# Parts of four layer 1 weight chunks made in layer 0 and kept in memory

## The chip, the cores and the metric

One core of a Trainium2 chip runs the kernel. The metric is device microseconds of one execution; lower is better. The kernel before takes 521.77 us, the median of three runs (521.5 to 522.45).

## The reference

Two residual layers over x of 512 tokens by 1024 channels, in fp32. What matters here:

```python
# layer 0: FoX (8 heads with a forget-gate bias) and MoBA (8 heads), head width 64
h = rms_norm(x, norm_g);  proj = h @ w_in          # q, k, v of both, forget logits, gate
logits = q k^T / 8 + c[query] - c[key]             # FoX: c is the running sum of log-sigmoid forget gates
out = softmax(masked logits) v                     # causal; MoBA: own block and chosen blocks
x = x + (concat(out_fox, out_moba) * silu(gate)) @ w_out
# layer 1: conformer convolution
val, glu, z = split(rms_norm(x, g) @ w_in, 3)      # 1024 channels each
u = causal depthwise conv of width 31 over (val * sigmoid(glu)), plus bias
x = x + (silu(layer_norm(u)) * silu(z)) @ w_out
```

## The kernel before

Each dense product is made in fp32 quality from split operands: a weight chunk of 1024 x 256 (1 MB) is held as hi, rounded to fp32r, and lo, the rest, and PE runs three passes (hi hi, hi lo, lo hi). There are 36 weight chunks in one list. Chunks 0 to 15 are layer 0's q, k, v and gate, 16 to 19 its output projection, 20 to 27 are layer 1's value and GLU gate, 28 to 31 its z, 32 to 35 its output projection, used in the order 33, 34, 32, 35.

`fetch(i)` loads a chunk by SP's queue into one of two buffers `wst` (L152). `split(i)` makes hi and lo: in most chunks of layer 0 ACT copies to hi (L173) and DVE or Pool subtracts in eight pieces (L177). In chunks named in `DMAS`, lo is made by an ACT negation of the whole chunk (L175) and a DMA on Pool's queue that accumulates the raw chunk into it (L179); in chunks named in `CAST`, hi is a casting DMA on Pool's queue (L169). Only Pool's queue casts or accumulates here. hi and lo go to `whi` and `wlo` (two buffers each), or to `wx` (four buffers). Chunk 32, the late one, has its lo in the place `gh` (L160, L161), and its hi is loaded with a cast by Pool's queue near the end (L1051). `ahead(n)` splits the next chunk and then fetches the next.

Layer 0 runs dense work (64 units: one token tile of a q, k or v chunk, or half of a gate chunk) between 64 attention tiles: 8 pairs of heads, of which pairs 0 to 3 are MoBA and 4 to 7 FoX, each with 2 heads and 4 query tiles. A tile is s (two matmuls, L510 and L512), p with bias and row maximum on DVE (L522), exp on ACT (L523), transposes on PE (L526) and copies back by ACT or DVE (L534, L536). A pair ends with the matmuls by v (L603) and a product with the reciprocal sums `rb`, which come back through memory (L546, L549, L608). A FoX head's bias tile `cb`, 128 x 512, is loaded by SP (L582) into one of two buffers and its diagonal pieces are masked by Pool (L518). Gate chunks end with a tanh (L626) and two DVE products (L623, L627). `ot` holds the attention's output, eight slots of 128 x 512; `e` is the tanh's buffer.

Layer 1 convolves tile by tile: of the 31 taps DVE takes most (L766), and the rest are a product on ACT (L775) that Pool adds (L776); L783 joins the two sums, PE transposes (L796), DVE gathers statistics (L798, L903, L904), Pool takes a power for the LayerNorm (L905 lnr), DVE normalises (L911 ctok), and PE transposes again (L922) ahead of the output projection. `POOLT` is the number of taps of ACT and Pool by channel block of 128 x 512, for blocks 0 to 5; `POOLH` the same for half tiles of blocks 6 and 7. z chunks run on PE (L370 to L372) meanwhile.

The order of instructions on each engine is fixed when the program is built, by a scheduler that goes by its own estimates of cost; each engine then runs its list in order, waiting on semaphores.

## Time and profile before

| | before |
|---|---|
| median of the runs | 521.77 us (521.5 to 522.45) |
| profiled execution, time and span | 522.39 us, 520.6 us |
| PE busy | 503.7 us, 97% |
| DVE busy | 373.0 us, 72% |
| ACT busy | 329.1 us, 63% |
| POOL busy | 232.6 us, 45% |
| moved by DMA | 79.05 MB |

The page gives busy time and, by line and shape, groups of instructions with the idle time ahead of them and the instruction that ended it. Stretches of time show which engine is full where; a timeline lists one engine's instructions with start, length and, in brackets, idle time ahead and its releaser. Here is the span in 40 equal slices of 13 us; a digit is tenths of a slice, a 9 being 90% or more:

```profile
PE   8999999999999999999999999999999999769997
DVE  7745677676465577596685256999999997868741
ACT  4945678777645775576384735998676765377230
POOL 5264852020422233223101113879988985687200
DMA  8742222302122242402219668488999799962111
```

PE's lower digits stand at about 440 to 470 us; Pool and the DMA engines are little used in the first half (layer 0) and full in layer 1.

### The profile page before, as it was taken

Reading aid. Unit: us, or ns where it says so; the run is one execution under the profiler, and the core shown is the slowest. Engines: PE = TensorE matmul, PEld = TensorE weight load, DVE = VectorE, ACT = ScalarE, POOL = GpSimd, SP = SyncE. Lnnn points to the kernel's source line nnn. Section 1 sums busy time; section 2 is a strip of 40 time slices with the busy share of each in tenths; the row PEclk is TensorE's granted clock in tenths of the full one; section 3 lists DMA queues with packets and bytes.
Section 4 is the critical chain, followed back from the end, with each engine's and each line's share of the span. In section 5 each row is a group of like instructions: output and inputs, shape, how many; then the busy total and the mean of one; then the engine's idle time right before and its main releaser. Section 6 shows DMA issues by size and latency. Waiting matters only on the chain.

```text
span 520.6 us, 9754 instructions
## 1 busy us (share of the span) xinstructions
PE 503.7 (97%) x3694; PEld 459.9 (88%) x3694; DVE 373.0 (72%) x788; ACT 329.1 (63%) x668; POOL 232.6 (45%) x255
## 2 busy tenths in 40 slices
PE   8999999999999999999999999999999999769997
...
DVE  7745677676465577596685256999999997868741
ACT  4945678777645775576384735998676765377230
POOL 5264852020422233223101113879988985687200
...
DMA  8742222302122242402219668488999799962111
GB/s 293 318 145 81 84 81 83 102 24 83 61 102 94 82 111 99 144 14 108 102 52 395 130 205 242 82 211 286 235 306 259 212 270 305 262 170 105 41 51 42
DMA packets 16566, 79.05 MB, mean 152 GB/s; under 512 B 1988, under 2 KB 4352, under 8 KB 8712
## 3 DMA queue, kind: packets, MB, share of 16 engines
q1 hardware_dynamic: 12632, 51.08, 27.1%
q0 software_dynamic: 3744, 27.26, 22.0%
...
## 4 chain that ended last, share of the span: by engine, by line
PE 70%; DMA 8%; POOL 7%; ACT 6%; DVE 4%; issue 3%; SPq 0%; POOLq 0%; ACTq 0%
PE mm L361 29%; POOL pacc L776 6%; PE mm L370 6%; PE mm L371 6%; PE mm L372 6%; DMA wst<-in_w_dram 5%; PE st L361 4%; PE o L603 3%; PE tp L526 3%; PE o L361 2%; PE s L510 2%; PE s L512 2%; DMA wlo<-wst 1%; DMA xt<-in_xt_dram 1%; PE s L361 1%
## 5 line engine op out<-in xcount | busy, mean ns | idle before, releaser
L776 POOL TENSOR_TENSOR pacc<-pacc,tm 128x256 f32<-128x256 f32 (+1 forms) x125 | 120.7, 986 | 15.8 <-ACT tm L775 10.1
L766 DVE SCALAR_TENSOR_TENSOR s<-u,parts,s 128x256 f32<-128x256 f32 (+1 forms) x211 | 108.1, 569 | 0.5
L361 PE MATMUL mm<-wlo,hhi 128*128 128x256 f32 (+1 forms) x352 | 98.7, 287 | 0.8 <-DVE wlo L177 0.5
L361 PE MATMUL mm<-whi,hhi 128*128 128x256 f32 (+1 forms) x352 | 98.4, 287 | 0.0
L361 PE MATMUL mm<-whi,hlo 128*128 128x256 f32 (+1 forms) x352 | 98.3, 286 | 0.0
L775 ACT ACTIVATE tm<-u,parts 128x256 f32<-128x256 f32 (+1 forms) x125 | 66.2, 571 | 14.5 <-POOL pacc L776 14.0
L361 PEld LDWEIGHTS mm<-wlo,hhi 128*128 128x128 f32 x352 | 65.8, 190 | 2.0 <-DVE wlo L177 0.8
L361 PEld LDWEIGHTS mm<-whi,hhi 128*128 128x128 f32 x352 | 65.6, 189 | 0.7 <-issue 0.2
L361 PEld LDWEIGHTS mm<-whi,hlo 128*128 128x128 f32 x352 | 65.9, 190 | 0.2
L177 POOL TENSOR_TENSOR wlo<-wst,whi 128x512 fp32r<-128x512 f32 (+1 forms) x22 | 31.0, 1423 | 57.4 <-ACT whi L173 57.4
L173 ACT ACTIVATE whi<-wst 128x512 fp32r<-128x512 f32 (+2 forms) x77 | 49.4, 707 | 5.9 <-DMA wst<-in_w_dram 2.7
L518 POOL TENSOR_TENSOR cb<-cb,mask 128x128 f32<-128x128 f32 x32 | 15.5, 490 | 80.7 <-DVE nm L522 46.2
L523 ACT ACTIVATE p<-p,nm 128x128 f32<-128x128 f32 (+3 forms) x64 | 35.7, 559 | 24.1 <-DVE nm L522 23.6
L177 DVE TENSOR_TENSOR wlo<-wst,whi 128x512 fp32r<-128x512 f32 (+1 forms) x50 | 39.8, 830 | 9.0 <-PE o L361 7.1
L370 PE MATMUL mm<-nhi,wx 128*128 128x256 f32 (+1 forms) x104 | 33.0, 318 | 0.0
L371 PE MATMUL mm<-nlo,wx 128*128 128x256 f32 (+1 forms) x104 | 32.2, 309 | 0.0
L372 PE MATMUL mm<-nhi,wx 128*128 128x256 f32 (+1 forms) x104 | 31.9, 307 | 0.0
L371 PE MATMUL mm<-nlo,whi 128*128 128x256 f32 (+1 forms) x104 | 31.8, 307 | 0.0
L372 PE MATMUL mm<-nhi,wlo 128*128 128x256 f32 (+1 forms) x104 | 31.7, 306 | 0.0
L370 PE MATMUL mm<-nhi,whi 128*128 128x256 f32 (+1 forms) x104 | 31.7, 307 | 0.0
L526 PE MATMUL tp<-identf,p 128*128 128x128 f32 x160 | 28.4, 275 | 1.1 <-ACT p L523 0.7
L396 POOL TENSOR_TENSOR rq<-vq,mhalf 128x16 f32<-128x16 f32 x8 | 26.2, 3272 | 6.2 <-DVE vq L394 6.1
...
## 6 DMA issues: line engine op xcount, KB each, us to landing
wst<-in_w_dram SPq DMA_DIRECT2D x33, 1024.0 KB, 5.0
wx<-wst POOLq DMA_DIRECT2D x13, 1024.0 KB, 7.2
wlo<-wst POOLq DMA_DIRECT2D x8, 1024.0 KB, 8.4
whi<-wst POOLq DMA_DIRECT2D x3, 1024.0 KB, 4.5
...
```

What stands on the lines that cost most here:

```text
L173: A.activation(hi[:, ks], st[:, ks], AF.Copy)
L177: (V if eng is G and parts == 4 and k % 4 and V0 else eng).tensor_tensor(lo[:, ks], st[:, ks], hi[:, ks].bitcast(F32), op=ALU.subtract)
L361: T.matmul(po, a[:, k, ts], b[:, k, :n], start=first and i == 0, stop=last and i == len(prods) - 1)
L370: T.matmul(po, whi[:, k, cs], a, start=k == 0, stop=False)
L371: T.matmul(po, whi[:, k, cs], b, start=False, stop=False)
L372: T.matmul(po, wlo[:, k, cs], a, start=False, stop=k == KC - 1)
L396: G.tensor_tensor(r, v, mhalf[:, :16].rearrange("p (t h) -> p t h", t=NT), op=ALU.pow)
L523: A.activation(p[:, :w], p[:, :w], AF.Exp, bias=nm, scale=-1.0, accum_out=sm[:, h, t:t + 1])
L526: T.transpose(tp[:, j * P:(j + 1) * P], p[:, j * P:(j + 1) * P], identf)
L766: V.scalar_tensor_tensor(acc[:, o], v, w, first[0][:, :n] if i == 1 else acc[:, o], op0=ALU.mult, op1=ALU.add)
L775: A.activation(tm[:, :n], v, AF.Copy, scale=w)
L776: G.tensor_tensor(pacc[:, o], pacc[:, o], tm[:, :n], op=ALU.add)
```

## The change

Chunks 30 to 33 (`PRE`) are no longer fetched and split in layer 1. In layer 0 each of them is taken in four quarters of 128 x 512, 16 in all, in 18 steps (`quarters`): a step is taken when the dense unit count reaches the next entry of `UNITS`, from 20 to 40. Step n issues, all on Pool: for item n - 2 the subtraction raw - hi and two DMAs that store hi and lo to memory (`pre`), and for item n two DMAs that load the quarter raw and cast to fp32r. The first instruction of a step is made to depend on ACT's evacuation of the last dense unit (`unit[0]`), and the others are chained behind it. The steps use three pairs of places in turn: two pairs of slots of `ot`, and a pair with the tags `e` (one buffer) and `cb` (two buffers). Altogether 16 subtractions and 64 DMAs of 256 KB are added to Pool's list in layer 0.

In layer 1, SP loads the ready hi and lo by plain DMAs of 1 MB each (`load_part`). 34 and 35 follow 29 in the order of fetches. 32's hi is now loaded by SP, too. `POOLT` gives blocks 2 to 5 one tap more on ACT and Pool each, so DVE has four taps of 128 x 512 less.

```diff
--- before.py
+++ after.py
@@ -29,9 +29,9 @@
 BIG = 1e30
 WC = 256
 WPAD = 260
-POOLT = [10, 11, 12, 11, 10, 11]
+POOLT = [10, 11, 13, 12, 11, 12]
 POOLH = {(6, 0): 10, (7, 0): 10, (6, 1): 16, (7, 1): 15}
-DMAS = (20, 21, 22, 23, 24, 25, 26, 27, 28, 29, 30, 31, 32, 33, 34, 35)
+DMAS = (20, 21, 22, 23, 24, 25, 26, 27, 28, 29, 34, 35)
 APARTS = 1
 TMB = 6
 NU = 3
@@ -66,9 +66,13 @@
     return nc.vector
 
 
-CAST = (22, 26, 27, 28, 30, 31, 33, 34, 35)
+CAST = (22, 26, 27, 28, 34, 35)
 PB = 4
 PTB = 4
+
+
+PRE = range(30, 34)
+UNITS = (20, 22, 24, 25, 26, 27, 28, 29, 30, 31, 32, 33, 34, 35, 36, 37, 38, 40)
 STK = 1
 PTS = 3 * P
 NLATE = 2
@@ -154,12 +158,6 @@
 
     def split_w(w, ring, eng, parts, cast):
         st, n = w
-        if ring == "late":
-            lo = l1p[0].tile([P, KC * WC], F32R, tag="gh", name="lo", bufs=1)
-            lo = lo.rearrange("p (k n) -> p k n", k=KC)
-            A.activation(lo, st, AF.Copy, scale=-1.0)
-            G.dma_start(lo.bitcast(F32), st, accum_op=ALU.add)
-            return None, lo
         if ring == "main":
             hi, lo = flat(main, F32R, "whi", n, 2), flat(main, F32R, "wlo", n, 2)
         else:
@@ -225,11 +223,28 @@
     raw, wts = {}, {}
 
     def fetch(i):
-        if i < len(wsrc):
+        if i < len(wsrc) and i not in PRE:
             raw[i] = load_w(*wsrc[i], 4 if i == 0 else 1)
 
+    pre = {i: dram.tile([2, P, KC * WC], F32, name=f"pre{i}") for i in PRE}
+
+    def load_part(i, j, x):
+        SY.dma_start(x.bitcast(F32).rearrange("p k n -> p (k n)"), pre[i][j])
+        return x
+
+    def load_parts(i):
+
+        if rings[i] == "late":
+            lo = l1p[0].tile([P, KC * WC], F32R, tag="gh", name="lo", bufs=1)
+            return None, load_part(i, 1, lo.rearrange("p (k n) -> p k n", k=KC))
+        pool, tags, bufs, wide = (main, ("whi", "wlo"), 2, WPAD) if rings[i] == "main" else \
+            (l1p[0], ("wx", "wx"), 4, WC)
+        return tuple(load_part(i, j, flat(pool, F32R, tags[j], WC, bufs, wide)) for j in range(2))
+
     def split(i):
-        if i < len(wsrc):
+        if i in PRE:
+            wts[i] = load_parts(i)
+        elif i < len(wsrc):
             wts[i] = split_w(raw.pop(i), rings[i], SPLIT_ENG(i, nc), APARTS if i in DMAS else 4 if i == 0 or 17 <= i < 24 else WPARTS, i in CAST)
 
     fetch_xt(0, 2)
@@ -372,6 +387,8 @@
+    unit = [None]
@@ -384,7 +401,7 @@
             po = mmbank() if i > 1 or t < 2 else sbank() if i == 0 else stbank() if t == 2 \
                 else bank("o", 1)
             tok_mm(po[:, :WC], WC, hhi, hlo, t, w, i == 0)
-            A.activation(raw_t[:, t, :], po[:, :WC], AF.Copy, scale=rinv[:, t:t + 1])
+            unit[0] = A.activation(raw_t[:, t, :], po[:, :WC], AF.Copy, scale=rinv[:, t:t + 1])
             sq = sqs[:, t % 2]
             A.activation(sq, po[:, :WC], AF.Square, scale=rinv[:, t:t + 1])
             V.reduce_sum(ss[:, t, :], sq.rearrange("p (h d) -> p h d", h=4), axis=AX.X)
@@ -419,7 +436,8 @@
             tok_mm(po[:, :n], n, hhi, hlo, t, w)
             c0 = 0 if c == 0 else (260 if n == 260 else WC)
             m = min(n, 512 - c0)
-            A.activation(vt[grp][:, t, c0:c0 + m], po[:, :m], AF.Copy, scale=rinv[:, t:t + 1])
+            unit[0] = A.activation(vt[grp][:, t, c0:c0 + m], po[:, :m], AF.Copy,
+                                   scale=rinv[:, t:t + 1])
             if m < n:
                 V.tensor_scalar(zf[:, t, :], po[:, m:n], rinv[:, t:t + 1], None, op0=ALU.mult)
             if t == NT - 1 and n > m:
@@ -623,9 +641,42 @@
             V.tensor_tensor(g, po, rbc, op=ALU.mult)
 
             e = at.tile([P, S], F32, tag="e", name="e", bufs=1)
-            A.activation(e, g, AF.Tanh)
+            unit[0] = A.activation(e, g, AF.Tanh)
             V.scalar_tensor_tensor(g, e, 1.0, g, op0=ALU.add, op1=ALU.mult)
             yield
+
+    QC = KC * WC // 4
+    behind = mybir.DependencyInfo(mybir.DependencyClass.Sync, mybir.DependencyReason.DATA)
+
+    def quarters(places, parts):
+
+
+        on_way = []
+        for n, (i, q) in enumerate(parts + [(None, None)] * 2):
+            mine = []
+            def then(f, *a, **k):
+                with tc.issue_after(mine[-1].ins) if mine else nullcontext():
+                    mine.append(f(*a, **k))
+
+            if n >= 2:
+                i0, q0, st, hi = on_way.pop(0)
+                then(G.tensor_tensor, st, st, hi, op=ALU.subtract)
+                for j, x in enumerate((hi, st)):
+                    then(G.dma_start, pre[i0][j][:, q0 * QC:(q0 + 1) * QC], x)
+            if i is not None:
+                st, hi = places[n % 3]
+                src = w_ap(*wsrc[i], q * KC // 4, KC // 4)
+                then(G.dma_start, st, src)
+                then(G.dma_start, hi.bitcast(F32R), src)
+                on_way.append((i, q, st, hi))
+            tc.add_manual_dep(mine[0].ins, unit[0].ins.name, behind)
+            yield
+
+    steps = list(UNITS)
+    presplit = quarters(((ot[:, 0], ot[:, 1]), (ot[:, 2], ot[:, 3]),
+                         (at.tile([P, S], F32, tag="e", name="pst", bufs=1),
+                          at.tile([P, S], F32, tag="cb", name="phi", bufs=2))),
+                        [(i, q) for i in PRE for q in range(4)])
 
     def dense():
         for i, f, a in ((0, qk_chunk, (("moba", "q", 0), 0)), (1, qk_chunk, (("moba", "k", 0), 1)),
@@ -658,6 +709,9 @@
         while done < min(n, 64):
             next(dn, None)
             done += 1
+            if steps and steps[0] <= done:
+                steps.pop(0)
+                next(presplit)
 
     att = attention()
     total = 0.0
@@ -802,14 +856,15 @@
     def new_pacc():
         return l1.tile([P, S], F32, tag="pacc", name="pacc", bufs=2)
 
-    nf, nsp = [18], [17]
+    nsp = [17]
+    nf = [i for i in range(18, len(wsrc)) if i not in PRE]
 
     def ahead(n):
         while nsp[0] < n:
             split(nsp[0])
             nsp[0] += 1
-            fetch(nf[0])
-            nf[0] += 1
+            if nf:
+                fetch(nf.pop(0))
 
     with tc.issue_after(his[-2].ins):
         ahead(18)
@@ -1048,8 +1103,7 @@
             ng_l(0, k + 1)
             if p == C34:
                 hi = main.tile([P, KC, WC], F32R, tag="big", name="hi", bufs=3)
-                G.dma_start(hi.rearrange("p k n -> p (k n)"), w_ap(*wsrc[32], 0, KC))
-                wts[32] = hi, wts[32][1]
+                wts[32] = load_part(32, 0, hi), wts[32][1]
             if p in (1, 2):
                 ng_t(0, p + 1)
             for (c, t), po in zip(units, banks):
```

**What moves on Pool and SP in layer 0.** The first place is the start of FoX. Names: `cb<-cb,mask` is the mask of a bias tile, `rq` a normalisation of a q or k chunk, `wlo<-wst,whi` a weight split; `pre_98` and `pre_99` are the kept halves of chunks 32 and 33, `pst` and `phi` the third pair of places. POOL before, from the first cb mask on:

```order
L518 TENSOR_TENSOR cb<-cb,mask 128x128 x2
L177 TENSOR_TENSOR wlo<-wst,whi 128x520
L396 TENSOR_TENSOR rq<-vq,mhalf 128x16
L177 TENSOR_TENSOR wlo<-wst,whi 128x520
L177 TENSOR_TENSOR wlo<-wst,whi 128x512
L396 TENSOR_TENSOR rq<-vq,mhalf 128x16
L177 TENSOR_TENSOR wlo<-wst,whi 128x512
L518 TENSOR_TENSOR cb<-cb,mask 128x128 x6
L396 TENSOR_TENSOR rq<-vq,mhalf 128x16
L518 TENSOR_TENSOR cb<-cb,mask 128x128 x7
```

POOL after, about the second cb mask (the first stands some rows ahead, also between steps):

```order
L659 DMA ot<-in_w_dram 128x512 x2
L659 TENSOR_TENSOR pst<-pst,phi 128x512
L659 DMA pre_98<-phi 128x512
L536 TENSOR_TENSOR cb<-cb,mask 128x128
L659 DMA pre_98<-pst 128x512
L659 DMA ot<-in_w_dram 128x512 x2
L659 TENSOR_TENSOR ot<-ot 128x512
```

and the last two steps, with the third mask behind them:

```order
L659 DMA pre_99<-ot 128x512
L413 TENSOR_TENSOR rq<-vq,mhalf 128x16
L659 DMA pre_99<-ot 128x512
L659 DMA ot<-in_w_dram 128x512 x2
L659 TENSOR_TENSOR pst<-pst,phi 128x512
L659 DMA pre_99<-phi 128x512
L413 TENSOR_TENSOR rq<-vq,mhalf 128x16
L659 DMA pre_99<-pst 128x512
L659 TENSOR_TENSOR ot<-ot 128x512
L659 DMA pre_99<-ot 128x512 x2
L536 TENSOR_TENSOR cb<-cb,mask 128x128
```

The masks, which came two and six at a time, are now single ones between the steps, and phi's last store (`pre_99<-phi`) lies ahead of the next mask. On SP, before, from the write of the running sums (`cdram`) on:

```order
L461 DMA cdram<-ct 8x512
L582 DMA cb<-cdram 128x512 x2
L546 DMA sdram<-rt_1614 8x128
L549 DMA rb<-sdram 64x512 x2
L152 DMA wst<-in_w_dram 128x2048
L546 DMA sdram<-rt_2057 8x128
L549 DMA rb<-sdram 64x512 x2
L152 DMA wst<-in_w_dram 128x2048 x2
```

and after:

```order
L479 DMA cdram<-ct 8x512
L564 DMA sdram<-rt_1654 8x128
L600 DMA cb<-cdram 128x512
L567 DMA rb<-sdram 64x512 x2
L156 DMA wst<-in_w_dram 128x2048
L564 DMA sdram<-rt_2140 8x128
L567 DMA rb<-sdram 64x512 x2
L156 DMA wst<-in_w_dram 128x2048 x4
L600 DMA cb<-cdram 128x512
L156 DMA wst<-in_w_dram 128x2048
```

The second cb load has moved from beside the first to behind five weight loads; it waits for phi's last store, since phi uses the second buffer of that tag.

**What moves on PE at the end of layer 0.** Attention tiles are moved back behind dense work: tile 36 of 64 stands at matmul 1299 of PE's list before and at 1502 after. The last gate matmul (hhi and hlo by whi and wlo) is number 1779 before and 1724 after, and tile 55 starts at 1646 before and 1725 after. PE before, at the last tiles of pair 7:

```order
L370 MATMUL mm<-hhi,whi 128x512
L371 MATMUL mm<-hlo,whi 128x512
L510 MATMUL s<-k_84,q_82 128x256
L512 MATMUL s<-kl_86,q_82 128x256
L526 MATMUL tp<-identf,p 128x128 x2
L510 MATMUL s<-k_85,q_83 128x256
L512 MATMUL s<-kl_87,q_83 128x256
L526 MATMUL tp<-identf,p 128x128 x4
L372 MATMUL mm<-hhi,wlo 128x512
L370 MATMUL mm<-hhi,whi 128x512
L371 MATMUL mm<-hlo,whi 128x512
L372 MATMUL mm<-hhi,wlo 128x512
```

and after:

```order
L528 MATMUL s<-k_84,q_82 128x256
L530 MATMUL s<-kl_86,q_82 128x256
L544 MATMUL tp<-identf,p 128x128 x7
L528 MATMUL s<-k_85,q_83 128x256
L530 MATMUL s<-kl_87,q_83 128x256
L528 MATMUL s<-k_84,q_82 128x256
L530 MATMUL s<-kl_86,q_82 128x256
L544 MATMUL tp<-identf,p 128x128 x5
L528 MATMUL s<-k_85,q_83 128x256
L530 MATMUL s<-kl_87,q_83 128x256
L544 MATMUL tp<-identf,p 128x128 x4
L578 MATMUL tp<-identf,rx 128x128 x4
```

Before, matmuls of the last gate unit stand between the pieces; after, the last tiles follow each other alone, up to the transposes of the reciprocal sums (`rx`).

**What moves on Pool in layer 1 ahead of lnr.** POOL before, from the last tile of block 5 to lnr:

```order
L776 TENSOR_TENSOR pacc<-pacc,tm 128x256
L169 DMA whi<-wst 128x2048
L776 TENSOR_TENSOR pacc<-pacc,tm 128x256
L179 DMA wlo<-wst 128x2048
L169 DMA whi<-wst 128x2048
L776 TENSOR_TENSOR pacc<-pacc,tm 128x256
L179 DMA wlo<-wst 128x2048
L776 TENSOR_TENSOR pacc<-pacc,tm 128x256 x14
L169 DMA wx<-wst 128x2048
L776 TENSOR_TENSOR pacc<-pacc,tm 128x256
L179 DMA wx<-wst 128x2048
L905 TENSOR_TENSOR lnr<-lnv,mhalf 128x2
```

and after:

```order
L830 TENSOR_TENSOR pacc<-pacc,tm 128x256 x3
L167 DMA whi<-wst 128x2048
L830 TENSOR_TENSOR pacc<-pacc,tm 128x256
L177 DMA wlo<-wst 128x2048
L830 TENSOR_TENSOR pacc<-pacc,tm 128x256 x9
L167 DMA wx<-wst 128x2048
L830 TENSOR_TENSOR pacc<-pacc,tm 128x256 x2
L177 DMA wx<-wst 128x2048
L830 TENSOR_TENSOR pacc<-pacc,tm 128x256 x3
L960 TENSOR_TENSOR lnr<-lnv,mhalf 128x2
```

The cast and the accumulate of chunk 33 have gone, and those that are left belong to 34 and 35.

## Prediction

> **What bounds the kernel now.** I read the shares by engine first, then stretches of 20 us, then PE's gaps and the chains behind them. TensorE (PE) is the bound:
>
> ```profile
> PE 503.7 (97%) x3694; PEld 459.9 (88%) x3694; DVE 373.0 (72%) x788; ACT 329.1 (63%) x668; POOL 232.6 (45%) x255
> ```
>
> Where PE is not busy (columns: stretch, its length, busy time and instructions of PE, PEld, DVE, ACT, POOL, then PE's granted clock, DMA share, GB/s):
>
> ```profile
> 71.00:200.00 129.00, 128.30 (x1004) 117.14 (x1004) 84.95 (x195) 90.46 (x215) 32.62 (x32) 1.00 0.23 77
> 180.00:266.00 86.00, 85.42 (x500) 68.51 (x499) 63.06 (x138) 54.24 (x128) 24.59 (x30) 1.00 0.28 90
> 208.00:262.00 54.00, 53.57 (x277) 41.35 (x276) 37.94 (x82) 30.91 (x73) 14.28 (x19) 1.00 0.27 91
> 255.00:265.00 10.00, 9.43 (x53) 6.84 (x53) 7.82 (x19) 6.21 (x15) 0.00 (x0) 1.00 0.01 3
> 380.00:400.00 20.00, 20.00 (x173) 20.00 (x173) 20.00 (x33) 15.80 (x21) 18.47 (x16) 1.00 0.99 267
> 420.00:440.00 20.00, 20.00 (x93) 16.37 (x92) 19.52 (x48) 11.91 (x21) 13.82 (x16) 1.00 0.99 276
> 442.00:465.00 23.00, 15.39 (x64) 11.72 (x62) 16.27 (x36) 12.56 (x26) 17.01 (x24) 0.93 0.91 243
> ```
>
> Layer 0 (to about 265 us) has PE full and Pool a quarter busy. The one hole is 442 to 465: 7.61 us of PE idle, under a DMA system that was 0.99 full before. PE's gaps there (start, length, then in brackets the idle time ahead and what ended it), and the chain on POOL, ACT and DVE:
>
> ```profile
> 444.35 0.44 PE L796 MATMUL tp<-identf,pacc 128*128 128x128 f32 x2 [1.48 <-DVE pacc L783]
> 452.04 0.41 PE L796 MATMUL tp<-identf,pacc 128*128 128x128 f32 x2 [1.74 <-DVE pacc L783]
> 460.50 0.30 PE L922 MATMUL tp<-identf,ctok 128*128 128x128 f32 x1 [3.92 <-DVE ctok L911]
> 414.51 0.60 POOL L169 DMA_DIRECT2D wx<-wst  x1 [0.73 <-PE st L372]
> 434.93 0.60 POOL L169 DMA_DIRECT2D whi<-wst  x1 [4.34 <-DMA wst<-in_w_dram]
> 436.68 0.87 POOL L179 DMA_DIRECT2D wlo<-wst  x1 [0.38 <-ACT wlo L175]
> 456.02 0.60 POOL L169 DMA_DIRECT2D wx<-wst  x1 [4.47 <-DMA wst<-in_w_dram]
> 458.36 1.01 POOL L905 TENSOR_TENSOR lnr<-lnv,mhalf 128x2 f32<-128x2 f32 x1
> 434.47 1.92 ACT L175 ACTIVATE wlo<-wst 128x2048 fp32r<-128x2048 f32 x1 [5.29 <-DMA wst<-in_w_dram]
> 455.53 1.91 ACT L175 ACTIVATE wx<-wst 128x2048 fp32r<-128x2048 f32 x1 [6.85 <-DMA wst<-in_w_dram]
> 443.87 0.42 DVE L783 TENSOR_TENSOR pacc<-s,pacc 128x256 f32<-128x256 f32 x1 [3.68 <-POOL pacc L776]
> 453.52 0.17 DVE L904 TENSOR_SCALAR lnv<-mv 128x2 f32<-128x2 f32 x1
> 459.40 3.55 DVE L911 TENSOR_SCALAR ctok<-ctok,mv,lnr 128x512 f32<-128x512 f32 x4 [3.82 <-POOL lnr L905]
> ```
>
> The statistics stand ready at 453.69, but lnr starts only at 458.36: Pool was stopped at the cast of chunk 35, whose load had just landed. The stop of 4.34 us at chunk 33's cast held the taps that DVE's L783 waits for.
>
> **Layer 1, what goes.** Chunks 30, 31, 33 and 32 need no load buffer, no cast, no negation and no accumulate any more; 34 and 35 take the early load slots of 30 and 31. The cast of 31 stood at 414.51, so raw data in its slot, now 35's, should be there some 40 us before the stop at 456; 34's lie one slot earlier. Neither Pool stop (4.34, 4.47) should be left. Pool also loses, ahead of lnr, the cast and accumulate of 33, 0.60 + 0.87, the like of 30 and 31, and 32's accumulate: 3 x 1.47 + 0.87 = 5.3 us. It gains four taps in place of DVE:
>
> ```profile
> 403.40 1.32 POOL L776 TENSOR_TENSOR pacc<-pacc,tm 128x512 f32<-128x512 f32 x1
> L766 DVE SCALAR_TENSOR_TENSOR s<-u,parts,s 128x512 f32<-128x512 f32 x72 | 50.2, 742 | 0.0
> ```
>
> 4 x 1.32 = 5.3 us, so Pool's work is even and only its stops go. DVE, full at 380 to 400, loses 4 x 0.74 = 3.0 us and the 3.68 us wait, so L783 moves from 443.87 to about 437 to 438, ahead of PE, which needs it at 444.35 - 1.48 = 442.87. With no wait PE reaches the next transposes at 452.04 - 1.48 - 1.74 = 448.82; statistics and lnv take 1.5 us behind those (452.04 to 453.52), lnr 1.0, and L911's first quarter 0.9, so the first ctok is ready at about 452.3. PE reaches L922 at 460.50 - 1.48 - 1.74 - 3.92 = 453.36. So all of 7.61 can go. The clock of 0.93 in that stretch, worth 15.39 x 0.07 = 1.1 us or somewhat more behind 460, should go with the idling. Ceiling 9.5. I take **-8.5**, since DVE and Pool have no slack ahead and something of 1 us may stay. If only chunk 35's stop goes, it is the 3.92 us gap: **-4** is the other end. The plain loads of ready halves, 8 x 1 MB, replace 4 loads plus 8 transfers on Pool's queue:
>
> ```profile
> q1 hardware_dynamic: 12632, 51.08, 27.1%
> q0 software_dynamic: 3744, 27.26, 22.0%
> wst<-in_w_dram SPq DMA_DIRECT2D x33, 1024.0 KB, 5.0
> wx<-wst POOLq DMA_DIRECT2D x13, 1024.0 KB, 7.2
> ```
>
> 27.1% of 520.6 us for 51.08 MB is 2.8 us per MB, Pool's queue 4.2; so 4 x (2.8 + 2 x 4.2) = 45 us of DMA become 22, which helps the full stretch. They wait only for PE to leave a buffer; at 5 us each they land ahead of use.
>
> **Layer 0, what comes.** Sixteen subtractions and 64 DMA issues on Pool between units 20 and 40, about 71 to 200 us. The nearest rows:
>
> ```profile
> L177 POOL TENSOR_TENSOR wlo<-wst,whi 128x512 fp32r<-128x512 f32 (+1 forms) x22 | 31.0, 1423 | 57.4 <-ACT whi L173 57.4
> 134.36 0.43 POOL L518 TENSOR_TENSOR cb<-cb,mask 128x128 f32<-128x128 f32 x1 [19.25 <-DMA cb<-cdram]
> 135.09 0.43 POOL L518 TENSOR_TENSOR cb<-cb,mask 128x128 f32<-128x128 f32 x1 [0.30 <-PE s L512]
> 215.70 0.35 SPq L152 DMA_DIRECT2D wst<-in_w_dram  x1
> ```
>
> 16 x 1.42 + 64 x 0.6 = 61 us, beside 32.6 of 129: Pool has room for 94. Bounds of an issue: 0.60 and 0.87, so up to 78 us. The 16 MB cost 45 to 67 us of DMA time by the prices above, share 0.23 to about 0.7: no bound, but SP's weight loads get slower.
>
> The place matters more than the sum. phi has the tag of FoX's bias tile cb, which has two buffers. Before, both heads' cb of pair 4 are loaded at once and masked at 134.36 and 135.09. Now the second cb load waits on SP for phi's last store. On Pool that lies behind a cb mask that waits for DVE's tile (order above); walking the queue with unit times of before, I get that mask at 167 to 171, phi's last store at 186 to 190, the second cb masked at 198 to 203 instead of 135. The weight load that stands behind the held one on SP was issued at 215.70 before, so that delay costs nothing.
>
> PE's order has been written for this: tile 36 of 64 stands at matmul 1502 of the program instead of 1299, so 29 tiles come after it against 17 there before; and the last gate matmul is 1724 instead of 1779, so tiles 55 to 64 have no dense work among them. One tile on DVE, from these groups of 180 to 266 (busy us, mean ns):
>
> ```profile
> L522 DVE CUSTOM_DVE_ANT_0 p<-s,cb 128x128 f32<-128x128 f32 (+3 forms) x26 | 12.1, 469 | 5.8 <-PE s L512 3.0 <-PE tp L526 1.8 <-PE st L495 0.6
> L536 DVE COPY pt<-tp 128x384 f32<-128x384 f32 (+3 forms) x15 | 7.1, 472 | 1.1 <-PE tp L526 0.9
> L501 DVE SCALAR_TENSOR_TENSOR kl<-st,gsc,k 64x512 fp32r<-64x512 f32 x6 | 4.5, 748 | 2.7 <-ACT k L500 2.6
> L491 DVE SCALAR_TENSOR_TENSOR q<-st,gsc,q 64x512 fp32r<-64x512 f32 x4 | 3.0, 750 | 1.0 <-ACT q L490 0.9
> L545 DVE RECIPROCAL rt<-tp 8x128 f32<-8x128 f32 x3 | 2.8, 941 | 1.4 <-PE tp L543 1.4
> L522 DVE DVE_READ_ACCUMULATOR2_ANT nm<- 128x1 f32 x26 | 2.1, 82 | 0.0
> L608 DVE TENSOR_TENSOR ot<-o,rb 128x512 f32<-128x512 f32 x3 | 2.1, 692 | 6.9 <-DMA rb<-sdram 6.9
> L676 DVE TENSOR_TENSOR ot<-ot,graw 128x512 f32<-128x512 f32 x7 | 4.8, 687 | 0.1
> ```
>
> 33.7 us over 26 tiles is 1.3 us a tile. Twelve more tiles in 208 to 262 add 15.6 to DVE's 37.9: 53.5 of 54, less some 5 us of gate work that now lies earlier. It just fits, with little slack. In the end piece, matmuls 1725 to 1797, PE has 73 x 85.42/500 = 12.5 us; DVE has 10 x 1.3 + 4 x 0.69 = 15.8, plus some of the wait for rb (6.9 in three, so 2.3 each): 18.1. That is 5.6 us, against 0.57 lost in 255 to 265 before. I take **+5**. Lower end -1: both heads' tiles overlap well enough, and the loss of before goes. Upper end +12: tiles run one after the other at up to 2 us each, and the rb wait stands twice: 20 + 2.8 + 4.6 - 12.5 = 14.9, which I cut since two heads alternate.
>
> [...]
>
> ```profile
> L398 DVE TENSOR_TENSOR qk<-qk,rq x8: 1225/2300/2327, 31.3 to 205.1; 128x1024 f32<-128x1024 f32 x8
> ```
>
> (min, median, max ns.) Sixteen subtractions that each cost DVE up to 1.1 us are 17.6 in 129 us where DVE has 44 free: 0 on the path, and 0 to +1 kept in the range. [...]
>
> **How the numbers follow.** -8.5 + 5 = -3.5. The profiled execution took 522.39 (span 520.6), 0.62 over the median of 521.77; on the median's scale **518.3**.
>
> **Rivals.** (a) Slower: the FoX tiles pushed together behind the held cb buffer cost more than the hole gives back, +9 to +12 against -8.5 or less: 523 to 526. It decides once the end piece loses over 8.5 us. For it: PE has had no spare work among its last ten tiles, and DVE is near full. Against it: DVE is the bound there by only a few us. 0.3. (b) Layer 0 hides everything, PE simply does the same matmuls in another order: -8.5 to -9.5, 512 to 513.5. For it: PE's total work is unchanged and it was full with some 30% of DVE free; against: the ten bare tiles. 0.2. (c) The weight waits go, but the conv itself is what comes late, DVE and Pool both being full from 380: -4 and +5, about 521 to 523, on both sides of no change. 0.12. My forecast, 515.5 to 520.5, 0.38.
>
> The range from 511.8 to 526 leaves out little of these; the likeliest case's own is 515.5 to 520.5. Within 0.2% (1 us, about what a measurement can tell from no change) I put 0.08, half of (c) and the edge of (a); slower 0.32 (0.28 of (a), 0.04 of (c)), faster 0.6.
>
> **What would show it.** In the profile after: no idle time ahead of POOL L169 behind 400 us, PE gaps of 442 to 465 under 2 us with the clock near 1.00, L922's first transposes about 7 us earlier against the end of layer 0. In layer 0: the second cb mask near 198, PE gaps in the last 20 us of attention, released by DVE, ACT or rb, of about 5 us. I am wrong if PE also stalls before 200 us behind Pool (rq waiting behind a quarter), if the end piece is bound by PE, or if L783 still makes PE wait.

## The result, and the profile after

The changed kernel takes 528.88 us (median of 4 runs, 527.62 to 529.19) against 521.69 before: a ratio of 1.013, 95% interval 1.0111 to 1.015. It is slower by some 7 us, where 518.3 was forecast. The profiled execution took 528.81, its span 527.0.

Busy shares first, as on the page before: Pool has gained 55 us of work, PE 5 us for the same 3694 matmuls.

```profile
PE 508.7 (97%) x3694; PEld 462.4 (88%) x3694; DVE 379.9 (72%) x784; ACT 324.7 (62%) x668; POOL 287.8 (55%) x331
```

Then stretches, columns as before (length, busy time of PE, PEld, DVE, ACT, POOL, granted clock, DMA share, GB/s): six of layer 0 and its end, one of the hole of layer 1, which lies 14 us later now.

```profile
100.00:120.00 20.00, 18.73 (x145) 16.39 (x144) 10.71 (x30) 14.86 (x34) 12.72 (x17) 1.00 0.59 168
235.00:240.00 5.00, 2.77 (x17) 2.45 (x17) 4.94 (x14) 3.37 (x10) 1.41 (x3) 0.85 0.56 210
240.00:245.00 5.00, 5.00 (x22) 4.00 (x21) 4.69 (x11) 3.98 (x9) 1.35 (x3) 0.81 0.39 105
260.00:265.00 5.00, 2.78 (x15) 1.49 (x15) 3.57 (x10) 2.03 (x8) 1.28 (x3) 1.00 0.27 105
265.00:270.00 5.00, 5.00 (x25) 2.94 (x26) 1.38 (x5) 2.09 (x7) 0.85 (x2) 0.66 0.15 55
275.00:280.00 5.00, 4.58 (x22) 3.48 (x24) 5.00 (x10) 5.00 (x11) 0.00 (x0) 0.66 0.01 3
456.00:479.00 23.00, 20.80 (x123) 17.43 (x121) 20.93 (x50) 16.34 (x37) 16.59 (x22) 1.00 0.47 138
```

The hole of layer 1 is mostly filled: 20.80 of 23 us where 15.39 were busy, at a clock of 1.00 and a DMA share of 0.47 instead of 0.91. At the end of layer 0 there are new holes, and at or behind each of them a clock of 0.66 to 0.85. These means hide what happens: in this trace the granted clock is 0.50 for 3.4 us at a time, and 1.00 in the stretches between (8 to 238.5, 242 to 265.8, 269.3 to 276 and 279.6 to 527). The three spells of 0.50 lie at the end of layer 0:

```profile
238.50:241.90 3.40, 3.22 (x12) 2.74 (x13) 3.12 (x9) 2.48 (x8) 0.00 (x0) 0.50 0.78 263
265.80:269.20 3.40, 3.40 (x18) 1.91 (x15) 0.57 (x4) 1.41 (x4) 0.85 (x2) 0.50 0.20 74
276.10:279.50 3.40, 3.40 (x17) 2.56 (x17) 3.40 (x6) 3.40 (x8) 0.00 (x0) 0.50 0.02 5
```

In the third spell the dense matmuls of 128 x 256 (L376) start every 0.21 us (276.90, 277.11, 277.32), behind it every 0.12 us (281.86, 281.98, 282.09). From this and the granted 0.50 I estimate that a spell costs a full PE 1.5 to 1.7 of its 3.4 us; below it is counted as 1.7. The kernel before has one such spell, from 461.4 to 464.8 in layer 1's hole, apart from its last 1.2 us.

The following table is worked out from the traces: PE does the same matmuls in both kernels, so the start of its n-th matmul says how far a kernel is behind or ahead of the kernel before, wherever the same matmuls lie ahead of it. That holds in these columns to within a few matmuls, except in `early` at 800 to 1254. Matmuls are counted as the trace records them, which is some 50 to 60 more by the end of layer 0 than in the program's list (the last gate matmul is 1840 before and 1777 after, against 1779 and 1724). Each row is one profiled execution; that of `two_places` was 5.4 us faster than its median, that of `hold_alone` 2.0 us slower. Differences to before in us (before's own times: 105.4, 118.4, 165.0, 282.0, 437.6, 481.7, 516.7):

| matmul of PE's list | 800 | 900 | 1254 | 2000 | 3200 | 3400 | 3690 |
|---|---|---|---|---|---|---|---|
| changed | +0.1 | +2.2 | +2.8 | +13.9 | +14.3 | +6.2 | +6.1 |
| l1_alone | +0.4 | +0.4 | +0.3 | +0.4 | +0.4 | -6.2 | -6.2 |
| l0_alone | -0.2 | +3.7 | +2.9 | +13.4 | +13.5 | +13.3 | +13.3 |
| two_places | +0.5 | +1.0 | +5.6 | +13.6 | +13.6 | +5.5 | +5.5 |
| early | +6.0 | +16.6 | +28.7 | +34.3 | +34.4 | +26.3 | +26.3 |
| small_bytes | +0.1 | +1.2 | +5.7 | +14.5 | +14.5 | +7.9 | +7.9 |
| hold_alone | +1.0 | +1.0 | +4.1 | +13.5 | +13.5 | +5.3 | +5.3 |
| hold_no_reload | -0.1 | -0.1 | +4.0 | +9.8 | +9.8 | +1.7 | +1.6 |
| bytes_alone | +0.4 | +3.2 | +12.1 | +12.3 | +13.2 | +7.6 | +7.6 |
| changed_no_rb | +0.5 | +0.8 | +3.2 | +11.9 | +11.9 | +3.7 | +3.7 |
| before_no_rb | +0.5 | +1.8 | +2.2 | +2.9 | +2.9 | +2.3 | +2.3 |
| two_chunks | -0.2 | +5.3 | +4.5 | +4.6 | +4.6 | -1.1 | -1.1 |
| two_chunks_no_rb | +0.5 | +0.8 | +3.6 | +5.1 | +5.2 | -2.1 | -2.1 |
| two_chunks_skip | +0.5 | +1.7 | +2.3 | +2.3 | +2.3 | -5.0 | -5.0 |
| one_chunk_look | +0.2 | +0.2 | +0.4 | +7.5 | +7.5 | +2.9 | +2.9 |

One execution of `one_chunk_quiet`, the one with its profile, took 816.67 us at a clock of 0.56, so its row is from `one_chunk_look`, the same kernel in another execution.

In the changed kernel layer 0 loses 2.8 us by matmul 1254 and another 11.2 by matmul 2000; layer 1 gives 8.1 back between 3200 and 3400.

The early loss, in DVE's and PE's timeline of the changed kernel:

```profile
116.29 0.69 DVE L626 TENSOR_TENSOR ot<-o,rb 128x512 f32<-128x512 f32 x1 [3.61 <-DMA rb<-sdram]
117.82 0.39 PE L376 MATMUL mm<-whi,hhi 128*128 128x256 f32 x1 [1.27 <-DVE zf L442]
```

DVE stands 3.61 us before a product that needs rb; behind it, in DVE's order, is zf, which frees an accumulator bank that PE wants.

The late loss: PE's two largest gaps, what DVE did ahead of the first, and the chain of the second one on SP, POOL and DVE.

```profile
236.72 0.39 PE L528 MATMUL s<-k,q 128*128 128x256 f32 x1 [1.91 <-DVE nm L540]
264.35 0.44 PE L528 MATMUL s<-k,q 128*128 128x384 f32 x1 [1.82 <-DVE nm L540]
232.61 3.12 DVE L175 TENSOR_TENSOR wlo<-wst,whi 128x512 fp32r<-128x512 f32 x2 [0.20 <-ACT whi L171]
235.65 0.68 DVE L626 TENSOR_TENSOR ot<-o,rb 128x512 f32<-128x512 f32 x1
236.25 0.41 DVE L540 CUSTOM_DVE_ANT_0 p<-s,cb 128x256 f32<-128x256 f32 x1
259.53 0.89 SPq L600 DMA_DIRECT2D cb<-cdram  x2
263.13 0.42 POOL L536 TENSOR_TENSOR cb<-cb,mask 128x128 f32<-128x128 f32 x1 [6.30 <-DMA cb<-cdram]
263.59 0.69 DVE L540 CUSTOM_DVE_ANT_0 p<-s,cb 128x512 f32<-128x512 f32 x1 [1.40 <-POOL cb L536]
```

At the first gap no load is late. DVE is full, 4.94 of the 5 us from 235 to 240: two weight subtractions, which take 1.4 and 1.8 us beside two of Pool's (each of four took under 0.7 us in the kernel before, from 229.7 on, without Pool's), and a product stand ahead of the tile that PE waits for.

At the second gap it is a load. The last tiles of pair 6 give the bias buffers back at about 259.4; SP loads the next at 259.53, Pool masks it 3.6 us later, DVE goes on at 263.59 and PE at 264.35, with no dense matmul left to put there.

In layer 1 the three waits of L796 and L922 on the weights' chain have gone; what is left at L922 is 0.48:

```profile
468.03 0.98 PE L977 MATMUL tp<-identf,ctok 128*128 128x128 f32 x7 [0.48 <-DVE ctok L966]
445.66 0.59 POOL L167 DMA_DIRECT2D whi<-wst  x1 [1.12 <-PE mm L387]
457.25 0.59 POOL L167 DMA_DIRECT2D wx<-wst  x1 [0.44 <-PE st L387]
```

(L977 is L922 of before, L167 the cast L169.)

### The profile page after: what moved, and what is told of

It reads as the page before. It is cut to its first block, busy times and chain, and to the rows that moved or that the text cites. A ratio compares the mean times of both kernels' runs of the same rounds, so it can differ in the third digit from the quotient of the medians.

```text
span 527.0 us, 9854 instructions
## 1 busy us (share of the span) xinstructions
PE 508.7 (97%) x3694; PEld 462.4 (88%) x3694; DVE 379.9 (72%) x784; ACT 324.7 (62%) x668; POOL 287.8 (55%) x331
## 4 chain that ended last, share of the span: by engine, by line
PE 81%; DVE 7%; DMA 4%; issue 2%; ACT 2%; POOL 2%; SPq 1%; POOLq 0%; DVEq 0%; ACTq 0%
PE mm L376 29%; PE mm L385 8%; PE mm L387 8%; PE mm L386 8%; PE st L376 5%; PE o L621 3%; PE st L385 2%; PE tp L544 2%; PE st L387 2%; PE st L386 2%; PE o L376 2%; PE s L376 2%; POOL pacc L830 2%; PE s L528 2%; DMA rb<-sdram 2%
## 5 line engine op out<-in xcount | busy, mean ns | idle before, releaser
L830 POOL TENSOR_TENSOR pacc<-pacc,tm 128x256 f32<-128x256 f32 (+1 forms) x129 | 125.3, 982 | 18.3 <-ACT tm L829 11.0
L820 DVE SCALAR_TENSOR_TENSOR s<-u,parts,s 128x256 f32<-128x256 f32 (+1 forms) x207 | 106.0, 567 | 0.7
L376 PE MATMUL mm<-whi,hhi 128*128 128x256 f32 (+1 forms) x352 | 98.8, 288 | 1.4 <-DVE zf L442 1.3
L376 PE MATMUL mm<-wlo,hhi 128*128 128x256 f32 (+1 forms) x352 | 98.1, 285 | 1.2 <-DVE wlo L175 0.9
L376 PE MATMUL mm<-whi,hlo 128*128 128x256 f32 (+1 forms) x352 | 98.4, 286 | 0.0
L829 ACT ACTIVATE tm<-u,parts 128x256 f32<-128x256 f32 (+1 forms) x129 | 68.5, 576 | 12.5 <-POOL pacc L830 11.9
L376 PEld LDWEIGHTS mm<-whi,hhi 128*128 128x128 f32 x352 | 65.7, 190 | 2.5 <-DVE zf L442 1.5
L376 PEld LDWEIGHTS mm<-wlo,hhi 128*128 128x128 f32 x352 | 65.8, 190 | 1.9 <-DVE wlo L175 1.1
L376 PEld LDWEIGHTS mm<-whi,hlo 128*128 128x128 f32 x352 | 65.8, 190 | 0.4 <-issue 0.2
L171 ACT ACTIVATE whi<-wst 128x512 fp32r<-128x512 f32 (+2 forms) x77 | 49.3, 707 | 14.5 <-PE mm L386 9.8
L175 DVE TENSOR_TENSOR wlo<-wst,whi 128x512 fp32r<-128x512 f32 (+1 forms) x50 | 44.2, 922 | 13.3 <-PE o L376 7.1
L175 POOL TENSOR_TENSOR wlo<-wst,whi 128x512 fp32r<-128x512 f32 (+1 forms) x22 | 31.0, 1419 | 12.5 <-ACT whi L171 12.4
L407 DVE TENSOR_REDUCE ssq<-sqs 128x4 f32<-128x256 f32 x32 | 13.2, 415 | 22.3 <-ACT sqs L406 21.7
```

The lines of the kernel that those rows point to most:

```text
L171: A.activation(hi[:, ks], st[:, ks], AF.Copy)
L175: (V if eng is G and parts == 4 and k % 4 and V0 else eng).tensor_tensor(lo[:, ks], st[:, ks], hi[:, ks].bitcast(F32), op=ALU.subtract)
L376: T.matmul(po, a[:, k, ts], b[:, k, :n], start=first and i == 0, stop=last and i == len(prods) - 1)
L820: V.scalar_tensor_tensor(acc[:, o], v, w, first[0][:, :n] if i == 1 else acc[:, o], op0=ALU.mult, op1=ALU.add)
L829: A.activation(tm[:, :n], v, AF.Copy, scale=w)
L830: G.tensor_tensor(pacc[:, o], pacc[:, o], tm[:, :n], op=ALU.add)
```

## The experiments

**The two halves.** `l1_alone` leaves the quarters out, so its weights for chunks 30 to 33 are not the right ones; `l0_alone` leaves layer 1 as before. Here and below the edits are shown abridged.

```diff
# l1_alone
-                next(presplit)
+                pass
-        SY.dma_start(x.bitcast(F32)..., pre[i][j])
+        SY.dma_start(x.bitcast(F32)..., pre)      # one chunk stored once, at chunk 2
# l0_alone
-POOLT = [10, 11, 13, 12, 11, 12]
+POOLT = [10, 11, 12, 11, 10, 11]
-        if i < len(wsrc) and i not in PRE:
+        if i < len(wsrc):
```

> Layer 1's part alone: the 16 quarters of layer 0 are left out; one 1 MB store of a layer 0 chunk stands in for what is kept, and the eight layer 1 loads read that (so the weights of chunks 30 to 33 are not those of the reference). PE's order in layer 0 is that of before. Both theories: layer 0 as before, layer 1 about 8 us shorter as in the changed kernel: 513.5 us (512.5 to 515). If layer 1's gain in the changed kernel were only layer 0's loss made good by waiting less, it would stay at 520 to 522.

Measured: 516.3 us, ratio 0.9872 (0.9835 to 0.9908). This is above the expected range: layer 1 gives 6.6 us back, where the changed kernel has 8.1. The 1.5 us between them are the clock. Between matmuls 3200 and 3400 PE's gaps cost 3.7 us in both, but in this execution a spell of half clock follows them, from 459.3 to 462.7, and in the changed kernel's none. The stretch to compare with 456 to 479 above, with the same 20.80 us of busy time:

```profile
442.00:465.00 23.00, 20.80 (x108) 17.44 (x107) 19.36 (x45) 14.68 (x33) 15.86 (x21) 0.93 0.47 138
```

> Layer 0's part alone: the 16 quarters run and are stored, but layer 1 loads, splits and uses chunks 30 to 33 as before, with the taps of before; nobody reads what is kept. Both theories: the changed kernel's +13.9 us at the end of layer 0 and nothing back: 535.5 us (534 to 537).

Measured: 535.16 us, ratio 1.0241 (1.0205 to 1.0276), +13.4 us at matmul 2000 and nothing back. The halves are separate: what the forecast missed lies in layer 0.

**Where the quarters lie.** `two_places` takes the bias buffer out of it, `early` starts ten units sooner.

```diff
# two_places (and steps one ahead, one unit fewer)
-                         (at.tile([P, S], F32, tag="e", name="pst", bufs=1),
-                          at.tile([P, S], F32, tag="cb", name="phi", bufs=2))),
-                st, hi = places[n % 3]
+                st, hi = places[n % 2]
# early
-UNITS = (20, 22, 24, ..., 38, 40)
+UNITS = (10, 12, 13, ..., 27, 28)
```

> The changed kernel with two pairs of places, both in ot, loads one step ahead and 17 steps, so no quarter uses the bias tile's buffer; Pool's 16 subtractions and 64 DMAs stay. PE's order is within a few matmuls that of before (tile 36 at 1300, last gate matmul at 1779). Theory A (the held bias buffer pushes the FoX tiles together, and that costs about 11 of the 13.9 us): layer 0 loses 2 to 4 us, from late rb loads, 516 us (515 to 518). Theory B (Pool's and the DMA queues' added work costs it, wherever the quarters lie): 10 us or more stay, 524 us or above.

Measured: 533.5 us (528.12 to 535.18), ratio 1.0187 (1.0121 to 1.0253). Theory A as I had put it fell: with PE's order of before, and the bias buffer free, layer 0 still lost 13.6 us, but elsewhere: 5.6 by matmul 1254, and 6.2 between 1600 and 1700, where quarters still ran beside FoX. There a product into `ot` waited, not for rb, but for the store of a quarter that lay in its slot:

```profile
236.28 0.69 DVE L626 TENSOR_TENSOR ot<-o,rb 128x512 f32<-128x512 f32 x1 [2.70 <-DMA pre<-ot]
237.03 1.07 PE L621 MATMUL o<-pt,v 128*64 128x512 f32 x2 [2.53 <-DVE ot L626]
```

So this kernel traded one lent place for another.

> The changed kernel with three pairs of places, but the 18 steps at units 10 to 28 instead of 20 to 40, so that the bias buffer is free again about when FoX first needs it. Tile 36 stands at matmul 1321, the last gate matmul at 1774. Theory A: layer 0 loses 3 to 6 us (the early MoBA tiles move back a little), 516 to 520 us. Theory B: Pool's work falls where it also splits weights for PE, so it costs as much or more: 526 us or above.

Measured: 550.19 us, ratio 1.0521 (1.0485 to 1.0556): 34 us lost in layer 0, with seven waits of DVE for rb that add up to 37.6 us, the longest 10.4. The kernel before has six, 13.8 us, beside a full PE.

**Bytes, hold, order.** These have layer 1's part of `l1_alone`, with its stand-in weights, so 516.3 us is their floor.

```diff
# small_bytes: each DMA 32 of 512 columns
+                src = bass.AP(tensor=w.tensor, offset=src.offset, ap=[src.ap[0], [1, 32]])
+                then(G.dma_start, st[:, :32], src)
# hold_alone: no quarters, last step at unit 46
+            if n in (2, 17):
+                then(G.memset, places[2][1][:, :1], 0.0) if n == 2 else then(G.dma_start, ..., places[2][1][:, :1])
# bytes_alone: ACT's queue, no cast, no subtraction
-                then(G.dma_start, st, src)
+                then(A.dma_start, st, src)
```

> Layer 1's part as in l1_alone (stand-in for the kept halves), and layer 0's 16 subtractions and 64 DMA issues on Pool in the same steps and places, but each DMA moves 128 x 32 instead of 128 x 512 (the rest of the places is set to zero once, and what is kept is not the reference's). PE's order is close to the changed kernel's: tile 36 at 1495, last gate matmul at 1704. Theory C (bytes: the small transfers rb, cb and the sums wait among the quarters' 16 MB): layer 0 loses 3 us or less, about 518 to 519 us. Theory D (order: the FoX tiles stand together without dense work, since the bias buffer is held and Pool's list is longer): about 10 us stay, 526 us. In both, l1_alone's 516.3 is the floor.

Measured: 530.72 us, ratio 1.0168 (1.0137 to 1.0198). With a sixteenth of the bytes the late loss is 8.8 us (5.7 to 14.5): theory C cannot explain that one. Nor can it explain the 5.7 us that are gone by matmul 1254, twice the changed kernel's 2.8.

> Layer 1's part as in l1_alone, and of layer 0's part only the hold: the second bias buffer is taken at unit 24 by one tiny memset and given back behind unit 46 by one tiny store; no subtraction, no quarter. PE's order is close to the changed kernel's (tile 36 at 1441, last gate matmul at 1724, the last nine tiles alike). Theory D: 8 to 11 us on top of 516.3, 525 to 527 us. Theory C: within 2 us of 516.3, 517 to 518.5 us.

Measured: 525.91 us (523.05 to 527.89), ratio 1.0061 (1.0033 to 1.0088). No quarter is moved and nothing subtracted, and yet 9.4 us go between matmuls 1254 and 2000, against 11.2 in the changed kernel: theory D for most of the late loss. Two things differ. It has no gap where the changed kernel has its first (236.72), so that one is read from the trace alone. And 4.1 us are gone by matmul 1254, 2.0 of them at one gap at 146.6 behind DVE's normalisation of a chunk: without a quarter, more can be lost early than the changed kernel lost. The last gap follows the same chain, and the clock behind it falls:

```profile
261.45 0.43 POOL L537 TENSOR_TENSOR cb<-cb,mask 128x128 f32<-128x128 f32 x1 [5.90 <-DMA cb<-cdram]
260.00:265.00 5.00, 3.03 (x9) 1.25 (x10) 3.56 (x10) 1.78 (x5) 1.93 (x5) 0.71 0.21 73
265.00:270.00 5.00, 5.00 (x27) 3.12 (x24) 0.35 (x1) 1.32 (x5) 0.20 (x1) 0.61 0.15 54
```

> Layer 1's part as in l1_alone, and of layer 0's part only the transfers, issued by ACT's queue without cast and without the subtraction: 64 DMAs of 256 KB in the same steps and places. Pool's list is free; PE's order is nearly that of before (tile 36 at 1312, last gate matmul at 1779). Theory C: rb and cb come late as in the changed kernel and in two_places, 522 to 528 us. Theory D: 517 to 519 us.

Measured: 529.21 us, ratio 1.0132 (1.0105 to 1.0159). Here 12.1 us go before matmul 1254 and next to nothing behind. DVE's waits for rb add up to 21.4 us by matmul 1254, against 6.9 before; here are three of the four, and in the last line a wait of ACT's:

```profile
117.66 0.69 DVE L627 TENSOR_TENSOR ot<-o,rb 128x512 f32<-128x512 f32 x1 [4.99 <-DMA rb<-sdram]
143.82 0.69 DVE L627 TENSOR_TENSOR ot<-o,rb 128x512 f32<-128x512 f32 x1 [5.40 <-DMA rb<-sdram]
167.09 0.69 DVE L627 TENSOR_TENSOR ot<-o,rb 128x512 f32<-128x512 f32 x1 [8.00 <-DMA rb<-sdram]
171.84 0.48 ACT L440 ACTIVATE v<-mm,rinv 128x260 f32<-128x260 f32 x1 [4.86 <-DMA pst<-in_w_dram]
```

That line shows what the edit adds of its own: the DMAs now stand in ACT's list, ACT waits for quarters with its own work behind, and PE waited 1.68 us for ACT at 172.37. So 12.1 us is not the price of the bytes alone. What the runs show is that the hold is enough for a loss of this size without a quarter; that bytes alone are enough is not shown.

**Half the work.** `two_chunks` keeps only 30 and 33, with the taps of before.

```diff
-PRE = range(30, 34)
+PRE = (30, 33)
-UNITS = (20, 22, ..., 38, 40)
+UNITS = (20, 22, 24, 25, 26, 27, 28, 29, 30, 31)
```

> The changed kernel with only chunks 30 and 33 kept (8 quarters, 10 steps at units 20 to 31), the taps of before, and 31 and 32 made in layer 1 as before. PE's order from tile 32 on is that of before, since phi is given back before FoX needs its buffer. Layer 1 should give back 6 to 7 us (two load slots fewer are enough to bring 33's and 35's casts in time). Theory C: layer 0 loses 2 to 3 us by the end of unit 31 and nothing behind, 517 to 518.5 us. Theory D: layer 0 loses about 1 us, 516 to 517 us.

Measured: 521.8 us, ratio 0.9978 (0.9956 to 1.0). Layer 0 loses 4.6 us, more than either theory had, and all in one place: a gap of 3.44 us and, behind it, a spell of half clock from 119.6 to 123.0. SP's and DVE's rows of this kernel, and SP's rows of before for the same transfers:

```profile
107.19 0.30 SPq L570 DMA_DIRECT2D sdram<-rt  x1
111.45 1.09 SPq L573 DMA_DIRECT2D rb<-sdram  x2
118.11 0.69 DVE L632 TENSOR_TENSOR ot<-o,rb 128x512 f32<-128x512 f32 x1 [5.78 <-DMA rb<-sdram]
119.64 0.58 PE L382 MATMUL mm<-whi,hhi 128*128 128x256 f32 x1 [3.44 <-DVE zf L448]
```

```profile
107.47 0.30 SPq L546 DMA_DIRECT2D sdram<-rt  x1
108.75 1.09 SPq L549 DMA_DIRECT2D rb<-sdram  x2
```

The store of 4 KB takes 4.3 us until rb can be issued, where before it took 1.3 (107.47 to 108.75); then the two loads of rb are there only at about 118.0, 6.6 us behind their issue, where before the product started 3.6 us behind it (112.38). The mean DMA share of layer 0 before, 0.23 in 71 to 200 us, says that there is room; while the loads of rb were on their way here, the share was 0.89 (the second line is the same stretch in `two_chunks_skip`, see below):

```profile
111.50:118.10 6.60, 4.70 (x36) 4.27 (x34) 0.57 (x2) 5.08 (x12) 4.32 (x5) 1.00 0.89 204
112.40:116.00 3.60, 3.60 (x29) 3.38 (x29) 0.57 (x3) 3.56 (x9) 1.05 (x1) 1.00 0.28 75
```

**Without the round trip.** A constant takes rb's place, in the changed kernel, in `two_chunks`, and in the kernel before as the control.

```diff
-        rb = at.tile([P, S], F32, tag="rb", name="rb", bufs=1)
-        for h in range(2):
-            SY.dma_start(rb[h * HD:(h + 1) * HD], sdram[i, h:h + 1].to_broadcast([HD, S]))
-        return rb
+        if not rb0:
+            rb0.append(at.tile([P, S], F32, tag="rb", name="rb", bufs=1))
+            V.memset(rb0[0], 1.0)
+        return rb0[0]
```

> The changed kernel with PE's order unchanged (tile 36 at 1502, last gate matmul at 1724), but the reciprocal sums rb are not fetched through memory: rb is a constant tile set once, so no product waits for the round trip (the division by the sums is left out). Theory E (two costs: the rb round trip held up by the quarters' bytes early in layer 0, about 2.8 us, and the FoX tiles without dense work behind the held bias buffer, about 11 us): the first goes, the second stays within 1 us, so 525 to 526.5 us. If bytes alone were behind all of it (theory C): 516 to 518 us. If order alone (theory D): 528 to 529 us.

Measured: 526.23 us, ratio 1.0062 (1.0044 to 1.0081), as theory E had it in total. The gap of 1.27 us at 117.8 is gone (+0.8 at matmul 900 instead of +2.2), but by matmul 1254 it is as far behind as the changed kernel, for another wait has come up (1.00 us behind rq, at 147.8). The late loss is 8.7 us instead of 11.2, more of a change than the 1 us expected. The two large gaps are still there (1.91 and 1.72 us); at the end of layer 0 this execution has one spell of half clock and not three.

> The control of the two others: the kernel before with the same constant in place of rb (the division by the sums is left out). Its rb waits of 13.8 us on DVE lie beside a full PE, so all theories: 520.5 to 522 us. If it is 2 us or more faster, that much of the others' gain is not the quarters' doing.

Measured: 524.98 us, ratio 1.0042 (1.0022 to 1.0063): the control is slower, by 2.3 us, outside what I expected. The scheduler makes another order without rb; that this order is what costs it is likely but not shown. So the two kernels without rb can be read only against it, and a couple of us in such a comparison prove little.

> two_chunks with the same constant in place of rb (the division by the sums is left out). Its layer 0 lost 4.6 us in one place, a gap of 3.45 us at 119.6 behind a product that waited 5.78 us for rb. Theory E: this goes, layer 0 as before or some 0.5 us better, layer 1 gives 5.7: 515.5 to 517.5 us. Theory D: 521 us or more. PE's order shifts a little (tile 36 at 1264 instead of 1299).

Measured: 522.06 us, ratio 0.9984 (0.9956 to 1.0012). The gap at 119.6 is gone (+0.8 at matmul 900 instead of +5.3), and 2.8 us come up behind it from other waits, the largest 1.20 us for rq at 145.5. The total decides nothing; the place does.

**What is left of the late loss.** `hold_no_reload` keeps the first pair's bias tiles for all FoX pairs.

```diff
-                    cb = at.tile([P, S], F32, tag="cb", name="cb", bufs=2)
-                    SY.dma_start(cb, cdram[hd:hd + 1, :].to_broadcast([P, S]))
+                    if len(kept) < 2:
+                        kept.append(at.tile([P, S], F32, tag="cb", name="cb", bufs=2))
+                        SY.dma_start(kept[-1], cdram[hd:hd + 1, :].to_broadcast([P, S]))
+                    cb = kept[h]
```

> hold_alone with the bias tiles of the first FoX pair used for all four pairs (the other heads' bias is left out), so that no reload of cb stands between a pair's last tile and the next pair's first; the second buffer is held to unit 46 as in hold_alone, and PE's order is the same up to tile 56 (tile 36 at 1441, last gate matmul at 1724). What is open: hold_alone loses 9.4 us behind matmul 1254, and its longest late gap (1.56 us at 262.7) follows a mask that waited for a reload. Theory F (the reload, exposed because the tiles stand bare, and the clock that falls behind it): 4 to 6 us less than hold_alone, 520 to 522 us. Theory G (tiles together without dense work are too slow on DVE and ACT whatever the loads do): 524.5 to 526 us.

Measured: 522.52 us, ratio 1.0005 (0.9986 to 1.0023), 3.4 us less than `hold_alone`. Between the theories: 3.6 of its 9.4 us go with the reload, but only 0.7 of them are time at gaps; 2.9 are pace, with two spells of half clock fewer at the end of layer 0 (one against three). 5.8 us stay with the bunched tiles.

**A version that beats both.** `two_chunks_skip` has no step at units 27 and 28.

```diff
-UNITS = (20, 22, 24, 25, 26, 27, 28, 29, 30, 31)
+UNITS = (20, 22, 24, 25, 26, 29, 30, 31, 32, 33)
```

> two_chunks with its ten steps at units 20, 22, 24, 25, 26, 29, 30, 31, 32, 33, so that no quarter is loaded or stored at units 27 and 28, when the second MoBA pair's sums go to memory and back. PE's order from tile 32 on is that of before. If the lost 4.6 us were that round trip, layer 0 loses 0.5 to 2 us now and the kernel takes 517 to 519 us; if another wait takes its place, 521 to 522 us.

Measured: 518.24 us (517.05 to 522.92), ratio 0.9928 (0.9903 to 0.9952). The same product waits 3.00 us instead of 5.78 and PE 0.66 instead of 3.44; layer 0 loses 2.3 us, a little more than expected, and layer 1 gives 7.3 back.

```profile
116.00 0.69 DVE L632 TENSOR_TENSOR ot<-o,rb 128x512 f32<-128x512 f32 x1 [3.00 <-DMA rb<-sdram]
117.53 0.39 PE L382 MATMUL mm<-whi,hhi 128*128 128x256 f32 x1 [0.66 <-DVE zf L448]
```

The work is the same and so is PE's order from tile 32 on; the steps of two units, and those behind them, come later. It mends half of the round trip: the loads of rb land 3.6 us behind their issue as before, but the store of 4 KB still takes 4.5 us (107.85 to 112.38), while quarters issued ahead of it were still moving (DMA share 0.74 in these us, against 0.02 in 107.47 to 108.75 before).

Of the 3.6 us between the two medians only 2.3 are this step. The rest is layer 1, where both kernels' gaps cost 4.6 to 4.7 us, but `two_chunks` had a spell of half clock behind them in its profiled execution, from 464.3 to 467.7, and `two_chunks_skip` none. The fastest execution of each, both at a mean clock of 1.00, took 519.21 and 517.05 us: 2.2 us.

**One chunk, in a quiet place.**

```diff
+PRE = (30,)
+UNITS = (36, 37, 38, 39, 40)      # two pairs of places, one step ahead
```

> A version that may beat both: one chunk, 30, kept; two pairs of places in ot, loads one step ahead, five steps at units 36 to 40, some 152 to 164 us, where no rb and no bias tile is on its way; phi is not used, and PE's order is nearly that of before (tile 36 at 1306, last gate matmul at 1783). The taps are those of before. Theory E: layer 0 loses 0 to 1 us; every later load in layer 1 moves one slot ahead, so chunk 33's and 35's casts stop Pool less: 4 to 6 us back. 516.5 to 518.5 us. If even four quarters cost what two_chunks lost: 520 to 522 us.

> The kernel of one_chunk_quiet again, for its profile, since the first look fell into a disturbed execution. From its times of 517.4 to 523.8 us: layer 0 loses 1 to 3 us, layer 1 gives 3 to 4 us.

Measured: 521.9 us, ratio 0.9967 (0.9942 to 0.9991), above the expected range; the one execution of `one_chunk_look` took 525.27, more than any of the other twelve. The place was not quiet. With loads only one step ahead Pool waits for them, and the bias masks wait behind:

```profile
174.05 1.30 POOL L665 TENSOR_TENSOR ot<-ot 128x512 f32<-128x512 f32 x1 [8.79 <-DMA ot<-in_w_dram]
182.39 1.28 POOL L665 TENSOR_TENSOR ot<-ot 128x512 f32<-128x512 f32 x1 [3.65 <-DMA ot<-in_w_dram]
184.69 0.42 DVE L546 CUSTOM_DVE_ANT_0 p<-s,cb 128x256 f32<-128x256 f32 x1 [3.54 <-POOL cb L542]
185.17 0.39 PE L534 MATMUL s<-k,q 128*128 128x256 f32 x1 [2.10 <-DVE nm L546]
```

It lost 7.5 us in layer 0 in that execution, where I had expected at most 3.

## Why the prediction was wrong

**Layer 1 was right, in size and mechanism.** Forecast -8.5, measured -8.1: 6.4 at gaps and 1.7 by a spell of half clock that did not come. By itself (`l1_alone`) it gave 6.6, with such a spell. L922 was to stand at 453.36 without waits; with layer 0's 14.3 us that is 467.7, and it stands at 468.03. Neither Pool stop of four us is left; the largest wait ahead of a cast is now 1.12 us.

**The held buffer was seen, and its time:** the second cb was to be masked at 198 to 203, and was at 202.15. That SP's weight loads behind it cost nothing held too.

**The step that failed is the +5 of layer 0, with its upper end of +12.** It priced the last ten tiles and nothing else. Measured +13.9, in three terms:

- Early, 2.8 us, where the sum had no term. "No bound, but SP's weight loads get slower" took the 16 MB by throughput. What came late at the early gap were short transfers: 4 KB of sums and the two loads of rb, for which DVE waits in order with PE's accumulator bank behind it. In sum the waits for rb did not even grow (6.7 us by matmul 1254, 6.9 before); one of them, 3.61 us where it had been 0.99, came where PE needed DVE. A row of before could have warned: the 6.9 us that L608 waited for rb, which I used for the end piece alone. What else is lost early in the kernels with another order (4.1 us in `hold_alone`, 5.7 in `small_bytes`) is not explained.
- Ahead of the end piece, 4.4 us, at the gap of 236.72 and the spell of half clock behind it. The sum had put this at nothing: DVE at 53.5 of 54 us in 208 to 262, less some 5 us of gate work, "just fits, with little slack". Such a mean hides a burst: in the five us from 235 DVE was busy 4.94 and came late with a tile, and dense matmuls stood behind the attention matmul that waited for it.
- In the end piece, 6.8 us against the forecast 5. I had 18.1 us for it, and it took 18.2 (258.33 to 276.54), but by luck. With each matmul at the median of its kind before, its PE work is 9.8 us and not 12.5. Of the other 8.4 us (1.6 at the same place of the list before), 5.0 are lost at gaps and 3.4 in pace. DVE was not the bound throughout: it stood 1.40 us for the reload of cb and then 3.64 for PE. The wait that I had put there, rb, was nothing. The reload stands in the list of waits of the trace of before (total, times, longest), beside dense work that hid it:

```profile
POOL cb L518 <- DMA cb<-cdram: 34.1, 6, 19.2
```

The clock had no term in layer 0. Between matmuls 1254 and 2000, by the same medians, 7.8 us are lost at gaps against 1.9 before, and 6.8 in pace against 1.4: 5.4 more, of which three spells of half clock, at the estimated 1.7 us each, explain 5.1. I had counted the clock in layer 1, where the hole of before ran at 0.93, and left it out where I made new holes.

That a subtraction on Pool costs DVE up to 1.1 us was my estimate from the spread of the L398 row; no run shows it for all sixteen. In the trace of before L398 took 1.23 us with no work of Pool's beside it (55.01) and 2.30 to 2.33 in the five executions beside one of Pool's weight subtractions. In the trace after, the same line (there L415) took 2.37 and 2.33 us beside two of the sixteen (190.46, 198.32) and one of DVE's weight subtractions 1.36 beside a third (88.86); but two of these took 1.29 together (182.83), the second of them beside the subtraction that Pool began at 183.63.

Rival (a) named the mechanism and its sign, and I gave it 0.3. It ended at +12 since I cut a worked upper end of 14.9 "because two heads alternate", which no row showed. That 14.9 lies near 13.9 is chance: it was the end piece's, which lost 6.8.

**Where the sum of the parts misleads.** `hold_alone` loses 13.1 us more than `l1_alone` at matmul 2000, `bytes_alone` 11.9, `small_bytes` 14.1, and the changed kernel, which has both hold and bytes, 13.5; by the medians of all executions it is 9.6, 12.9, 14.4 and 12.6. The costs don't add; `bytes_alone` has ACT's own stops in it, and one spell of half clock more or less moves any of these by an estimated 1.7 us.

**Open.** Nothing was taken out of the changed kernel that brought its 11.2 late us back: that the hold is behind them is shown by adding it alone, and the first gap is read from the trace. What share of the bunched tiles' 5.8 us in `hold_no_reload` is DVE and what ACT, and whether DVE's two subtractions slowed beside Pool made the first gap, was not tried.
